# One written order for the query, value and gate heads of a DeltaNet layer on a Trainium2 core

## The chip, the core and the metric

The kernel runs on one core of one Trainium2 chip. Times are device microseconds (us) of one execution. The kernel before was run three times: 1217.61, 1218.7 and 1219.78, median 1218.7. The profile is of one more execution, recorded by the hardware profiler.

A core has five engines that work side by side, each with a queue of instructions that it takes strictly in order: TensorE (PE, matmuls; the loading of its stationary operand is shown apart as PEld), VectorE (DVE), ScalarE (ACT), GpSimd (POOL) and SyncE (SP, which here only issues DMA transfers; ScalarE issues some too). They meet through semaphores: an instruction whose input is not ready waits, and so does everything behind it on its queue. SBUF is the on-chip memory, 128 partitions wide; PSUM holds the matmul results.

## The reference, cut to what matters

The whole program is two layers on 512 latent and 256 context tokens of width 1024 (`D_MODEL`): a bidirectional gated DeltaNet layer and an attention layer. Only a part of the first is touched. There, the normalised tokens are projected, a convolution of width 5 over the tokens and a SiLU follow for queries, keys and values, and a gate z is projected without a convolution:

```python
p = u @ w_in
qkv = jax.nn.silu(centred_dwconv(p[..., :DN_CONV_DIM], conv_w))
z = p[..., DN_CONV_DIM:DN_CONV_DIM + DN_VAL_DIM]
...
q = jnp.repeat(l2_norm(q.reshape(b, l, DN_QK_HEADS, DN_HEAD_K)), rep, axis=2)
k = jnp.repeat(l2_norm(k.reshape(b, l, DN_QK_HEADS, DN_HEAD_K)), rep, axis=2)
v = v.reshape(b, l, DN_V_HEADS, DN_HEAD_V)
```

There are 8 query heads, 8 key heads, 16 value heads and 16 gate heads of 128 columns each. Then, per value head, per direction and per chunk of 64 tokens:

```python
a = jnp.where(strict, jnp.einsum('bhncd,bhnsd->bhncs', kb, kc) * decay, 0.0)
t_inv = lax.linalg.triangular_solve(eye + a, jnp.broadcast_to(eye, a.shape),
                                    left_side=True, lower=True, unit_diagonal=True)
...
qk = jnp.einsum('bhncd,bhnsd->bhncs', qc, kc) * decay
...
def step(s, xs):
    qk_i, qd_i, kd_i, u_i, w_i, gl_i = xs
    v_new = u_i - jnp.einsum('bhcd,bhde->bhce', w_i, s)
    o = jnp.einsum('bhcd,bhde->bhce', qd_i, s) + jnp.einsum('bhcs,bhse->bhce', qk_i, v_new)
    s = s * gl_i[..., None, None] + jnp.einsum('bhcd,bhce->bhde', kd_i, v_new)
    return s, o
```

So `t_inv`, the inverse of a unit lower triangular 64x64 block, is needed for every chunk, value head and direction, and `qk` likewise. Both can be computed before the recurrence over chunks begins.

## The kernel before, in words

The program runs in stages: the modulated norm and the key heads (to about 167 us); the **stage of the change** (167 to 602 us), which computes the query, value and gate heads and, beside them, all block inverses and all masked query-key products; the recurrence over 12 chunk steps (`products`, `solve`, `update`, L889 to L985); the output projection, the attention layer and the last norm.

**One head.** A head is a GEMM of a 1024x128 weight slice with the 1024x768 token matrix. The 32-bit product is built from high and low parts: `wh` and `wl` of the weight, `uh` and `ul` of the tokens, and three products `wh*uh`, `wh*ul`, `wl*uh`. That makes 24 matmuls of 512 latent columns and 24 of 256 context columns for each head (`gemm_T`, L342; the matmul is L349). `load_w` (L324) loads the slice with a DMA on SP (L329), ScalarE casts it to `wh` (L330), and VectorE or POOL subtracts to get `wl` (L331). For query and value heads `conv_silu` (L361) makes the convolution from the PSUM result: ScalarE writes the middle tap (L368), VectorE adds four taps (L371) for the latent columns and four for the context columns, ScalarE takes a tanh and VectorE completes the SiLU: L382 writes `sil_q` in two pieces, with the chunks placed in pairs, L376 writes `sil_v`. A gate head has no taps, only tanh and one VectorE instruction per part.

What follows differs. A **query** head (`q_head`, L531) is squared by ScalarE (`sq_q`, L499), TensorE sums the squares (`ss_q`, L504), and the head is stored to the DRAM buffer `q_d`. A **value** head (`v_head`, L762) is transposed by TensorE to tokens, copied by ScalarE into `vt`, and stored to `v_d` by a DMA on ScalarE's queue; this "tail" is held back by two heads (`turn_tails`). A **gate** head (`z_head`) is stored to `z_d`.

**The block inverses.** The tokens form six tiles t = 0 to 5 of 128 rows, each a pair of 64-row chunks. All of this runs in 32x32 sub-blocks. Per tile:

- *masked products* (`t_masked`, L585): load the keys `kk` (from `k_d`, which the key heads stored, L529) and the decay rows `df`; ScalarE makes the decays with 16 small instructions (L581) and one exponential (L582) for each direction v = 0, 1; TensorE forms the products of the keys, `G` (L604); VectorE masks them into `Gx` (L606) and multiplies with the decays (L562): `md` for the diagonal sub-blocks (128 partitions) and `mo` for the off-diagonal ones (two instructions of 32 partitions). VectorE transposes `md` to `L` (L626), so that the heads and directions lie on the partitions.
- *solve* (`t_solve`, L669): for two tiles together POOL inverts the 32x32 triangles column by column: 31 columns, each a product into `tmp` (L682) and a subtraction from `X` (L683), 93 of each in all.
- *join* (`t_join`, L691): VectorE transposes `X` back to `U` (two instructions, L698), TensorE makes `pp` from `mo` and `U` (64 small matmuls, L704), ScalarE negates it into `pn`, TensorE makes `pw`, and ScalarE copies all into `Tt`, of which there are two buffers in turn, and which is stored to `t_d`.
- *queries* (`t_queries`, L632): the products `GQ` of keys and queries, masked by VectorE and multiplied with the decays by POOL (12 products of 128x1024, all on POOL), stored to `qk_d`.

**What sets the order.** The stage is placed by the Tile scheduler: the program text gives an order, `issue_after` adds "not before" conditions, and the scheduler fills the engines' queues. The head loop (L784 on) emits q0 to q7, then the string `"z" * 5 + "vvz" * 8 + "zzz"`. Weights are split up to three heads ahead, for query heads on POOL, for all others on VectorE. Beside the heads a generator `pieces()` yields pieces of the inverses and query products, of which one is taken per query head, two per value head and three per gate head.

**Behind the stage.** The recurrence's order is written by hand already. Its first step loads on SP, in this order, `cT` from `t_d`, four pieces of `cv` from `v_d` (L878), three pieces of `cQK`, and the keys `ckt`. The first update of the state is the matmul `su` (L969), which reads `ckt`.

## Time and profile before

| | before |
|---|---|
| median of three runs | 1218.7 us (1217.61 to 1219.78) |
| the profiled execution's own time | 1220.96 us |
| its span in the profile | 1219.2 us |
| granted TensorE clock, mean | 0.978 |
| busy share of the span: PE / PEld / DVE / ACT / POOL | 94% / 76% / 66% / 60% / 47% |
| bytes moved by DMA | 208.73 MB, mean 171 GB/s |

The profile is a page of views and a trace that can be asked for more. "Busy" is the time in which an engine executes; waits and DMA issues do not count. Engine names with a q (ACTq, SPq) stand for the issue of transfers from that engine's queue. In a group of instructions `x24` is their count, after it come busy time and mean duration in ns, and behind the next bar the idle time of the engine just before them with what ended most of it. In a list of single instructions the first number is the start, the second the duration, and a bracket gives the idle time before it. The clock is the share of full speed that TensorE was granted: 0.50 is half speed.

### The profile page before, as it was taken

The numbers are of one execution on the slowest core, as the hardware profiler recorded it, in microseconds if no ns is written. First come the engines' busy times: TensorE is split into PE (matmuls) and PEld (weight loads), VectorE is DVE, ScalarE is ACT, GpSimd is POOL, SyncE is SP. The second block draws the span as 40 slices with busy tenths as digits, with TensorE's granted clock in tenths as the row PEclk, the third lists the DMA queues.
The fourth block names the chain that finished last, engine by engine and source line by source line (L and its number), as shares of the span: only waits on it lengthen the run. The fifth ranks groups of instructions, "written<-read, shape, count | busy, mean of one in ns | idle before, by whom it ended". The sixth has DMA issues, their size and how long they took to land. (4 is left out here: it accounts for less than half of the span.)

```text
span 1219.2 us, 27757 instructions
## 1 busy us (share of the span) xinstructions
PE 1144.4 (94%) x10739; PEld 928.9 (76%) x10739; DVE 800.2 (66%) x1734; ACT 731.5 (60%) x1945; POOL 579.1 (47%) x442
## 2 busy tenths in 40 slices
PE   4999999999789989899999999899999999999996
PEld 1677678888678877788856666688887889999884
DVE  2688565777879645675478888635556566566646
ACT  3344336675565678896268999686663236666731
POOL 0131114229999999830067568455753344230810
PEclk9999899999899998899999999999999999999998
DMA  9465986454436569752999999266672202101323
GB/s 335 137 227 169 338 258 191 130 166 155 132 111 178 162 187 280 235 177 98 295 267 242 260 270 250 76 223 190 217 233 98 70 26 80 52 19 53 104 69 87
DMA packets 171125, 208.73 MB, mean 171 GB/s; under 512 B 12497, under 2 KB 126322, under 8 KB 170226
## 3 DMA queue, kind: packets, MB, share of 16 engines
q1 hardware_dynamic: 151346, 197.02, 53.8%
q10 hardware_dynamic: 19648, 9.94, 2.9%
q8 instruction: 85, 1.39, 0.5%
q14 instruction: 46, 0.38, 0.1%
HBM read 166.16 MB, written 40.67 MB: 170 GB/s over the span
## 5 line engine op out<-in xcount | busy, mean ns | idle before, releaser
L918 POOL TENSOR_TENSOR S<-S,glb 128x512 f32<-128x512 f32 x80 | 81.7, 1043 | 122.0 <-PE ks L909 122.0
L1076 PE MATMUL po<-woh,y 128*128 128x512 f32 x384 | 130.0, 403 | 0.7 <-ACT y L1052 0.7
L349 PE MATMUL g_v<-uh,wh 128*128 128x512 f32 (+1 forms) x256 | 91.4, 357 | 14.8 <-DVE sil_v L376 14.8
L1025 POOL TENSOR_TENSOR wol<-wo,woh 128x1024 fp32r<-128x1024 f32 x32 | 77.1, 2411 | 55.6 <-ACT woh L1018 52.7
L683 POOL TENSOR_TENSOR X<-X,tmp 128x62 f32<-128x62 f32 (+15 forms) x93 | 95.8, 1031 | 6.5
L371 DVE SCALAR_TENSOR_TENSOR acc_v<-g_v,cwv,acc_v 128x510 f32<-128x510 f32 (+3 forms) x128 | 74.5, 610 | 33.9 <-ACT acc_v L368 32.3
L349 PE MATMUL g_z<-uh,wh 128*128 128x512 f32 (+1 forms) x256 | 88.6, 346 | 5.7 <-DVE sil_v L376 5.7
L682 POOL TENSOR_TENSOR tmp<-L,X 128x62 f32<-128x62 f32 (+15 forms) x93 | 89.0, 957 | 6.9
L349 PE MATMUL g_v<-ul,wh 128*128 128x512 f32 (+1 forms) x256 | 89.6, 350 | 0.0
L349 PE MATMUL g_v<-uh,wl 128*128 128x512 f32 (+1 forms) x256 | 88.7, 346 | 0.0
L349 PE MATMUL g_z<-ul,wh 128*128 128x512 f32 (+1 forms) x256 | 87.3, 341 | 0.0
L349 PE MATMUL g_z<-uh,wl 128*128 128x512 f32 (+1 forms) x256 | 87.1, 340 | 0.0
L1076 PEld LDWEIGHTS po<-woh,y 128*128 128x128 f32 x384 | 72.5, 189 | 16.0 <-ACT y L1052 0.9
L1076 PE MATMUL po<-wol,y 128*128 128x512 f32 x192 | 75.7, 395 | 0.9 <-POOL wol L1025 0.9
L349 PEld LDWEIGHTS g_v<-uh,wh 128*128 128x128 f32 x256 | 50.6, 198 | 21.6 <-DVE sil_v L376 15.5
L331 POOL TENSOR_TENSOR wl_k<-w_k,wh_k 128x1024 fp32r<-128x1024 f32 x8 | 19.3, 2415 | 94.6 <-ACT wh_k L330 94.6
L331 POOL TENSOR_TENSOR wl<-w,wh 128x1024 fp32r<-128x1024 f32 x8 | 19.4, 2426 | 83.6 <-ACT wh L330 83.6
L349 PEld LDWEIGHTS g_z<-uh,wh 128*128 128x128 f32 x256 | 49.2, 192 | 11.6 <-DVE sil_v L376 6.4
L331 DVE TENSOR_TENSOR wl<-w,wh 128x1024 fp32r<-128x1024 f32 x32 | 49.9, 1560 | 11.6 <-ACT wh L330 11.6
L1050 DVE SCALAR_TENSOR_TENSOR pt<-pt,og,z 128x128 f32<-128x128 f32 x96 | 34.4, 358 | 34.7 <-PE pt L1041 31.9
L909 PE MATMUL ks<-S,ck 128*64 128x256 f32 x352 | 55.2, 392 | 0.4 <-ACT o L915 0.4
L983 DVE TENSOR_TENSOR S<-su,S 128x512 f32<-128x512 f32 x80 | 51.5, 686 | 6.0 <-PE su L969 3.9
(375 smaller groups left out, 3397.4 us busy)
## 6 DMA issues: line engine op xcount, KB each, us to landing
aw<-in_ada_w SPq DMA_DIRECT2D x24, 1024.0 KB, 7.3
w<-in_dn_w_in SPq DMA_DIRECT2D x40, 512.0 KB, 4.6
wo<-in_dn_w_out SPq DMA_DIRECT2D x32, 512.0 KB, 3.3
cv<-v_d SPq DMA_DIRECT2D x48, 256.0 KB, 8.0
df<-gc_d SPq DMA_DIRECT2D x48, 128.0 KB, 2.8
z_d<-zs SPq DMA_DIRECT2D x16, 384.0 KB, 5.8
v_d<-vt ACTq DMA_DIRECT2D x16, 384.0 KB, 4.0
t_d<-Tt SPq DMA_DIRECT2D x6, 1024.0 KB, 5.1
```

What stands on the lines that cost most here:

```text
L331: split_at[0] = E.tensor_tensor(wl[:, :, :m], w[:, :, :m], wh[:, :, :m], ALU.subtract).ins
L349: mm = T.matmul(pg_[:m, :n], w[:, k, :m], u[:, k, c0:c0 + n], start=k == 0 and n_ == 0, stop=k == KT - 1 and n_ == 2)
L371: V.scalar_tensor_tensor(acc[:, c0 + lo:c0 + hi], ps[:, lo + j - 2:hi + j - 2], cwv[:, j, ct:ct + 1], acc[:, c0 + lo:c0 + hi], ALU.mult, A ...
L682: E.tensor_tensor(tv, bcast(L[:, :, j + 1:, j], 3, j + 1), bcast(X[:, :, j, 0:j + 1], 2, n), ALU.mult)
L683: E.tensor_tensor(X[:, :, j + 1:, 0:j + 1], X[:, :, j + 1:, 0:j + 1], tv, ALU.subtract)
L909: T.matmul(ks[r0:r0 + 64, w], kq[w][:, hh, r0:r0 + 64], St[hh][:, d], start=True, stop=True)
L918: G.tensor_tensor(St[hh], St[hh], bcast(g_, 3, P), ALU.mult)
L983: V.tensor_tensor(St[hh], sj, St[hh], ALU.add)
L1025: G.tensor_tensor(wl, raws.pop(n), halves[n][0], ALU.subtract)
L1050: V.scalar_tensor_tensor(pj, pj, og, raw(z, off, [[st_, 2], [1, 64]]), ALU.mult, ALU.mult)
L1076: T.matmul(acc[:, nh], y[i][:, j, :], ww[k][:, nh * 512:(nh + 1) * 512], start=h == 0 and x == 0, stop=h == VH - 1 and x == 2)
```

## The change

The change replaces the scheduler's placement of this stage by an order that is written out for all five queues (`tc.manual_schedule` over TensorE, VectorE, ScalarE, GpSimd and SyncE). The arithmetic stays the same.

- Time is cut into **slots**, one per head. The new order of heads is `"zzzzzqqzqqzqqvqqvvzvvzvzvvzvvzvzvvzvvzvz"`: five gates first, then queries mixed with gates and values, the last three heads being z14, v15, z15 (before: three gates).
- In slot n the loop emits: the load of the weights of head n+3; planned loads; the store of head n-2; planned TensorE work (`pe`); the latent GEMM of head n; copies of head n-2; the end of head n-1 (context taps, both SiLU parts, for queries the square); the split of the weights of head n+2 (POOL while n < 4, VectorE after); the context GEMM of head n; the turn of head n-1 on TensorE (sums of squares or transposes); planned middle work (`mid`: masks, mask products, turns); some columns of the solve on POOL, by a budget of 8.6 per slot; the beginning of head n (latent taps); late planned work (decays).
- Both SiLU parts of a query or value head n-1 lie in slot n. A gate's latent part now comes before its context part, and lies in its own slot.
- The key products `G` of tiles 0 to 5 stand in slots 1, 2, 5, 8, 11, 13; `L` is turned at the slots in `TURNED`; `U` at 18, 21, 26, 29, 34, 37, with `pp` ahead of the GEMM one slot later and `pw` two slots later; query products in slots 19, 22, 25, 28, 31, 34.
- *Larger pieces of mask products:* for v = 0 the off-diagonal product `mo` is one instruction over all 128 partitions, of which v = 1 then overwrites the blocks 0 and 3 in two instructions as before. Per tile there are three `mo` instructions instead of four.
- Of the twelve query products those of tiles 0 to 2 stay on POOL; the six of tiles 3 to 5 go to VectorE.
- There is one `Tt` buffer instead of two, `U` is one tile instead of two, and the decay rows have four buffers of one kind.

```diff
-    for Tt in Tts:
-        for b in range(4):
...
+    def decay(t, v, first, last):
+
+        df = dfs[t, v]
+        for h in range(first, last):
             S.activation(df[:, h], df[:, h], AF.Abs, scale=-1.0, bias=gcV[:, v, t, h:h + 1])
-        S.activation(df, df, AF.Exp, scale=-1.0)
...
+        if last == VH:
+            S.activation(df, df, AF.Exp, scale=-1.0)
...
+    def m_prod(t, v):
...
+        df, Gx, mo, md = dfs.pop((t, v)), Gxs[t], mos[t], mds[t]
+        decayed(V, md[:, v], df[:, :, 0:32], Gx[:, :, 0:32])
+        for r in ((slice(0, P),), (slice(0, 32), slice(96, P)))[v]:
+            decayed(V, mo[r], df[r, :, 32:64], Gx[r, :, 32:64])
...
-                for b in ((1, 2), (0, 3))[v]:
-                    r = slice(b * 32, b * 32 + 32)
-                    decayed(V, mo[r], df[r, :, 32:64], Gx[r, :, 32:64])
...
+    order = "zzzzzqqzqqzqqvqqvvzvvzvzvvzvvzvzvvzvvzvz"
+    heads = [(c, order[:n].count(c)) for n, c in enumerate(order)]
...
+    def decay_at(s, t, v):
+        at_slot(s, "late", decay, t, v, 0, 12)
+        at_slot(s + 1, "mid", decay, t, v, 12, VH)
+
+    POOL_FROM = 4
+    TURNED = (3, 4, 10, 12, 15, 18)
+    for t, (s, p0, p1) in enumerate(((1, 2, 2), (2, 3, 4), (5, 7, 8), (8, 10, 11), (11, 13, 14), (13, 16, 17))):
+        if t >= 2:
+            at_slot(s - 1, "sp", keys_loaded, t, False)
+            for v in range(2):
+                at_slot(s - 1, "sp", decay_rows, t, v, True)
+                decay_at(s + v, t, v)
+        at_slot(s, "pe", m_gram, t)
+        at_slot(s, "mid", m_masks, t)
+        at_slot(p0, "mid", m_prod, t, 0)
+        at_slot(p1, "mid", m_prod, t, 1)
+        at_slot(TURNED[t], "mid", m_turn, t)
+    at_slot(0, "sp", keys_loaded, 0, False)
+    at_slot(1, "sp", keys_loaded, 1, False)
+    for n in range(4):
+        at_slot(0, "sp", decay_rows, n // 2, n % 2, True)
+        at_slot(n, "late", decay, n // 2, n % 2, 0, VH)
+    for t, s in enumerate((18, 21, 26, 29, 34, 37)):
+        at_slot(s, "mid", j_turn, t)
+        at_slot(s + 1, "pe", j_first, t)
+        at_slot(s + 1, "mid", j_mid, t)
+        at_slot(s + 2, "pe", j_second, t)
+        at_slot(s + 2, "mid", j_end, t)
+        at_slot(s + 3, "sp", lambda t=t: dma(t_d[t], Tt))
+    for t, s in enumerate((19, 22, 25, 28, 31, 34)):
+        at_slot(s - 1, "sp", keys_loaded, t, True)
+        for v in range(2):
+            at_slot(s - 1, "sp", decay_rows, t, v, False)
+        at_slot(s, "pe", q_gram, t)
+        at_slot(s, "mid", q_masks, t)
+        for v in range(2):
+            decay_at(s + v, t, v)
+            at_slot(s + 1 + v, "mid", q_prod, t, v, G if t < 3 else V)
+            at_slot(s + 2 + v, "sp", q_store, t, v)
...
+    def head_begun(n):
+        if heads[n][0] == "z":
+            squash(n, 0)
+            silu(n, 0)
+        else:
+            taps(n, 0)
+
+    def head_ended(n):
+        c, h = heads[n]
+        if c == "z":
+            squash(n, 1)
+            silu(n, 1)
+            return
+        taps(n, 1)
+        squash(n, 0)
+        silu(n, 0)
+        squash(n, 1)
+        silu(n, 1)
+        if c == "q":
+            sq = sums[n] = ap_.tile([P, NT, P], F32, tag="tok", name=f"sq_{c}{h}").rearrange("p t k -> p (t k)")
+            S.activation(sq, sils[n], AF.Square)
...
+    written_p = tc.manual_schedule(engines={T.engine, V.engine, S.engine, G.engine, nc.sync.engine})
+    written_p.__enter__()
+    for n in range(3):
+        w_load(n)
+        if n < 2:
+            w_split(n, G)
+    for n in range(N + 3):
+        p_ = plan[n]
+        if 3 <= n + 3 < N:
+            w_load(n + 3)
+        run(p_["sp"])
+        if 2 <= n < N + 2:
+            head_stored(n - 2)
+        run(p_["pe"])
+        if n < N:
+            gemm_part(n, 0)
+        if 0 <= n - 2 < N:
+            head_copied(n - 2)
+        if 0 <= n - 1 < N:
+            head_ended(n - 1)
+        if n + 2 < N:
+            w_split(n + 2, G if n < POOL_FROM else V)
+        if n < N:
+            gemm_part(n, 1)
+        if 0 <= n - 1 < N:
+            head_turned(n - 1)
+        run(p_["mid"])
+        solve_some(n)
+        if n < N:
+            head_begun(n)
+        run(p_["late"])
+        if n == N - 1:
+            run(rsqrt_steps(rq.rearrange("p t h -> p (t h)"), 1.0))
...
-    work = pieces()
-    ahead = set()
-    order = "z" * 5 + "vvz" * 8 + "zzz"
...
-    for n_, (f_, h) in enumerate(heads):
-        for g_, h_ in heads[n_:n_ + 3]:
-            c_ = column[g_] + h_
-            if (g_, h_) not in ahead:
-                ahead.add((g_, h_))
-                split_ahead(c_, f"{c_}", G if g_ is q_head else V)
-        at[0] = n_
-        f_(h)
-        with tc.issue_after(split_at[0]), tc.issue_after(split_at[1]), tc.issue_after(at[1]), tc.issue_after(done[-2][0]), tc.issue_after(done[-2][1]):
-            for _ in range({q_head: 1, z_head: 3, v_head: 2}[f_]):
-                next(work, None)
```

## What the change was predicted to do

> **What bounds the kernel now.** I read the page first (span, shares, slices), then the windows of the stage that the change rewrites, then the timeline at TensorE's gaps there. All times are in us.
>
> ```profile
> span 1219.2 us, 27757 instructions
> ```
> ```profile
> 166.90:296.60 129.70, 129.70 (x1145) 110.24 (x1144) 89.52 (x164) 81.68 (x220) 52.02 (x45) 1.00 0.60 173
> 296.60:602.00 305.40, 276.40 (x3254) 240.12 (x3256) 202.89 (x280) 202.07 (x501) 214.86 (x186) 0.96 0.59 182
> 360.00:400.00 40.00, 35.51 (x566) 31.18 (x566) 38.56 (x41) 23.53 (x46) 36.38 (x29) 0.96 0.54 149
> 366.00:369.40 3.40, 3.05 (x7) 2.47 (x8) 3.40 (x4) 2.21 (x4) 3.24 (x3) 0.50 0.86 228
> 505.90:512.70 6.80, 6.10 (x14) 4.79 (x15) 6.25 (x8) 5.47 (x19) 3.31 (x3) 0.50 0.68 219
> ```
> ```profile
> 506.60 0.79 PE L349 MATMUL g_v<-uh,wh 128*128 128x512 f32 x1 [3.12 <-DVE sil_v L376]
> ```
>
> A window's columns are its length, the busy time of PE, PEld, DVE, ACT and POOL, the granted clock, and DMA. TensorE bounds this stage: it is busy for all of 129.70 while the first 13 heads (q0 to q7, z0 to z4) run. Over the other 27 heads it idles 305.40 - 276.40 = 29.0, and 4% of the clock is missing, 12, part of it inside the gaps; I count 10. So 39 is all that a better order can win here. The reader is to see two more things: a gap waits for VectorE's silu (sil_v), and in the one window where VectorE is full (38.56 of 40) TensorE starves (35.51). The clock was 0.50 for 6.8 after the gap of 3.12.
>
> **The change part by part.** Every queue's order is now written. In slot n TensorE runs the GEMM of head n and, behind it, the turn of head n-1: the sums of a query's squares, or a value's transposes. VectorE runs the four taps of head n-1's context columns, its silu, the weights' subtraction for head n+2, the "mid" work (masks, mask products, turns), then the four taps of head n's latent columns (for a gate, one silu).
>
> *TensorE's work* keeps its amount:
>
> ```profile
> 197.08 0.39 PE L349 MATMUL g_q<-uh,wl 128*128 128x512 f32 x1
> 197.31 0.39 PE L349 MATMUL g_q<-uh,wh 128*128 128x512 f32 x1
> 199.06 0.28 PE L349 MATMUL g_q<-uh,wh 128*128 128x256 f32 x1
> 199.18 0.28 PE L349 MATMUL g_q<-ul,wh 128*128 128x256 f32 x1
> 206.53 0.87 PE L504 MATMUL ss_q<-ones,sq_q 128*64 128x1 f32 x24
> 287.06 1.10 PE L604 MATMUL G<-kk 128*32 128x64 f32 x64
> 518.66 1.29 PE L704 MATMUL pp<-U,mo 32*32 32x32 f32 x128
> ```
>
> From start to start a latent matmul takes 0.23 and a context one 0.12: a head is 24 x 0.228 + 24 x 0.12 = 8.35. With 0.8 for sums, about as much or a little less for transposes, 1.1 for a pair of G products and 1.25 for each join product, slots 5 to 18 hold 130.6 and slots 19 to 39 hold 205.4.
>
> *The start.* G of tile 0 now stands on TensorE straight behind z0 and the last key head's transposes (before, two query heads lay between), and all of z1 behind it. It needs k_d, which that key head's store completes.
>
> ```profile
> 181.42 1.02 DVE L518 TENSOR_TENSOR kt<-tr_k,kss 128x512 f32<-128x512 f32 x2
> 188.18 0.86 ACT L526 COPY kb<-kb 128x512 f32<-128x512 f32 x2 [0.55 <-PE kb L524]
> 189.07 0.37 ACTq L529 DMA_DIRECT2D k_d<-kb  x1
> 187.25 6.29 SPq L589 DMA_DIRECT2D kk<-k_d  x2
> DMA to landing us min/median/max: 2.7/4.6/5.1
> ```
>
> (The last row is that of tile kk.) kt is there at 182.4, z0 ends near 181.6 (where q0 ends now), the transposes near 183.2, the store goes out at 183.8. The second key load ended its issue at 187.25 + 6.29 = 193.5, 4.1 from the store's start at 189.07 to its own start; then 4.6 to land: 183.8 + 4.1 + 4.6 = 192.5, against a TensorE free at 183.2. Less G's own first half, 8.8 idle (2.7 to land gives 6.9; twice the store's time gives 13). A gap of that size halves the clock: 6.8 x 0.5 less what lies in the gap, 2.3 taken. Sum 11; z4 ends near 230. VectorE is nearly idle in these five slots: a gate head gives it one silu and, until head 5, POOL subtracts the weights.
>
> *Slots 5 to 18: query heads, masks and values.*
>
> ```profile
> 183.22 2.04 DVE L371 SCALAR_TENSOR_TENSOR acc_q<-g_q,cwv,acc_q 128x254 f32<-128x254 f32 x4 [0.78 <-ACT acc_q L368]
> L371 DVE SCALAR_TENSOR_TENSOR acc_q<-g_q,cwv,acc_q 128x511 f32<-128x511 f32 x12 | 8.9, 738 | 0.1
> 179.50 0.76 DVE L382 SCALAR_TENSOR_TENSOR sil_q<-g_q,acc_q 128x256 f32<-128x256 f32 x2
> 186.28 0.48 DVE L382 SCALAR_TENSOR_TENSOR sil_q<-g_q,acc_q 128x128 f32<-128x128 f32 x2
> L376 DVE SCALAR_TENSOR_TENSOR sil_v<-g_v,acc_v 128x512 f32<-128x512 f32 x16 | 10.9, 682 | 4.3 <-ACT g_v L374 4.2
> L376 DVE SCALAR_TENSOR_TENSOR sil_v<-g_v,acc_v 128x256 f32<-128x256 f32 x16 | 6.7, 419 | 3.4 <-ACT g_v L374 3.4
> L331 DVE TENSOR_TENSOR wl<-w,wh 128x1024 fp32r<-128x1024 f32 x32 | 49.9, 1560 | 11.6 <-ACT wh L330 11.6
> L499 ACT ACTIVATE sq_q<-sil_q 128x768 f32<-128x768 f32 x7 | 5.9, 836 | 0.5 <-DVE sil_q L382 0.5
> L330 ACT CAST wh<-w 128x1024 fp32r<-128x1024 f32 x35 | 36.5, 1043 | 7.1 <-PE g_v L349 4.1 <-DMA w<-in_dn_w_in 1.9 <-PE g_z L349 1.0
> L562 DVE TENSOR_TENSOR mo<-df,Gx 32x512 f32<-32x512 f32 x24 | 28.0, 1167 | 2.7 <-ACT Gx L607 2.4
> L562 DVE TENSOR_TENSOR md<-df,Gx 128x512 f32<-128x512 f32 x12 | 11.1, 928 | 6.1 <-ACT df L582 6.0
> L606 DVE TENSOR_TENSOR Gx<-G,masks 128x128 f32<-128x128 f32 x12 | 3.4, 283 | 0.8 <-PE G L604 0.8
> L626 DVE STREAM_TRANSPOSE L<-md 128x1024 f32<-128x1024 f32 x6 | 13.6, 2272 | 2.4 <-POOL tmp L682 2.3
> L698 DVE STREAM_TRANSPOSE U<-X 128x1024 f32<-128x1024 f32 x12 | 24.6, 2120 | 0.0
> L581 ACT ACTIVATE df<-df,gcV 128x64 f32<-128x64 f32 x189 | 47.5, 337 | 6.2 <-DMA df<-gc_d 6.2
> L582 ACT ACTIVATE df<-df 128x1024 f32<-128x1024 f32 x12 | 12.7, 1057 | 0.0
> ```
>
> A VectorE slot behind a query is 2.05 + 1.25 for taps and silu; then a wait of 2.0, since ScalarE's square (0.84) and the cast that the subtraction needs (1.04) both come after that silu; 1.56; the mid work M; 4 x 0.78 = 3.1. That is 10.1 + M. Behind a value the square is absent: 8.3 + M. Behind a gate: 5.5 + M. Where the current head is a gate, the last 3.1 is 0.7. M is 2.1 or 3.3 for a half of the mask products (the first of a pair as one instruction of 128 partitions, 0.93 + about 1.17; the three narrow ones were 1.17 each), 0.6 for masks, 2.3 for L, 4.2 for U. Slots 6 to 18 come to 147 (10.1, 9.8, 9.5, 10.1, 12.1, 9.5, 12.4, 12.8, 11.7, 12.4, 12.2, 11.7, 12.6); in slots 6 and 9 ScalarE's decays (12 x 0.25, then 4 and the exponential, 2.1) add 1.5 each: 150. TensorE needs 121. It lets VectorE run late by at most 3.6, as the square of head n-1 ends 4.75 into slot n and its sums are due at 8.35. So 29 - 3.6 = 25 of idle, 2 to 4 per slot from slot 10. If only VectorE's busy time counted, slots 10 to 18 would hold 95.6 against 83.1: 9.
>
> *The joins.* U is turned in slots 18, 21, 26, 29, 34, 37, and the first join product stands ahead of the next head's GEMM. From a value's silu it is 0.35 + 1.56 + 4.2 = 6.2 to U's end. With VectorE on time the silu ends 4.4 before the GEMM: 1.2 of wait; with VectorE just late enough, 5.6. In slot 18 L's 2.3 comes on top. Laid out slot by slot, ScalarE's 8 copies into Tt ahead of the next taps included, I get 7.9, 5.0, 3.3, 4.5, 3.3, 5.7: 30 (floor 9.5).
>
> *The end.* v15 is now the last head but one (now three gates follow it), and its transposes are TensorE's last work. Their rows must reach v_d and come back.
>
> ```profile
> v_d<-vt ACTq DMA_DIRECT2D x16, 384.0 KB, 4.0
> ```
> ```profile
> 583.93 1.98 SPq L878 DMA_DIRECT2D cv<-v_d  x2
> 604.22 1.04 PE L969 MATMUL su<-vd,ckt 64*64 64x256 f32 x16
> DMA to landing us min/median/max: 5.6/6.4/8.6
> ```
>
> (The last row is that of tile ckt.) On SP the last cQK and ckt stand behind the two loads of v_d[1]. With the stage's TensorE end at 230 + 130.6 + 25 + 205.4 + 30 = 621: copies 1.0, store 4.0, two loads' issue 2.0, a cQK issue 0.6, ckt 6.4: su starts at 635. Now it starts at 604.22.
>
> *The rest, at nothing.* POOL's columns (8 to 9 a slot, as planned) end some slots before U needs them; if not, U waits and the joins grow. Of POOL's twelve query products six go to VectorE, 1.8 each (twice md), in slots 29 to 36, inside the join sum; two subtractions more go there too, 3.1, in slots 4 and 5 where it is idle. SP loads each weight three slots ahead; one Tt buffer has at least two slots between its store and its next copy.
>
> **Sum.** 635 - 604 = +31 on the profiled execution of 1220.96 (span 1219.2), which lies 2.3 above the median 1218.7: 1250.
>
> By the Trainium skill, "TensorE: Matmul & The Clock Gate", Part 1, the clock falls after an idle window of about 3.4. Here 3.12 was enough. By that rule only four of the six join gaps would slow the clock, and the slow rival below would be 1259, not 1264.
>
> **The rivals.**
> - *Faster:* VectorE stays within its 3.6 of lateness, so the 25 goes and the joins fall to 9.5: 31 - 25 - 20.5 = -14, 1204. For it: 129.70 of 129.70 busy, with VectorE at 69%. Against it: 35.51 with VectorE at 96%, and the wait for the square, which the order fixes. It decides at a lateness of 3.6 in slots 10 to 18.
> - *Half:* the square's wait is hidden, 9 in place of 25, and the joins cost 20: +5, 1224.
> - *Clock:* each join gap also costs 2.3 of half clock that no lateness absorbs: +14 more, 1264. Against it: while VectorE is late, a slower TensorE only shortens the next wait.
> - *No change:* the terms meet the 39 exactly.
>
> **How the numbers follow.** Forecast 0.48 (its own range 1234 to 1260), half 0.21, clock 0.11, no change 0.03, faster 0.17. What measurement can tell from no change is about 0.2%. Slower 0.80, same 0.03, faster 0.17. Low end: 9 for 25, floor joins, a start of 9: 31 - 16 - 20.5 - 2 = -8, 1211. High end: clock, and a start of 15: 1269.
>
> **What would show it.** Right: TensorE idle about 9 before G of tile 0; sums of squares waiting for sq_q in slots 9 to 16, 2 to 4 each; join products waiting for U, 3 to 8 each; the first su near 635. Wrong: VectorE on time at slot 18 (z4's end plus 131), join gaps near 1, or G of tile 0 not waiting.

## The result, and the profile after

The changed kernel takes 1277.89 us in the median of four runs (1267.13 to 1281.11), the kernel before 1218.64. The ratio is 1.047 with a 95% interval of 1.0408 to 1.0533. The direction was forecast, the size was not: 1250 with a range of 1211 to 1269. The profiled execution took 1276.98, 56.0 longer in its span than that of the kernel before.

First the page of the changed kernel: span, busy time per engine, and the granted clock in 40 slices.

```profile
span 1275.2 us, 27658 instructions
PE 1156.2 (91%) x10739; PEld 940.4 (74%) x10739; DVE 816.1 (64%) x1736; ACT 732.8 (57%) x1945; POOL 554.6 (43%) x430
PEclk9999899999998998989879999999999999999998
```

TensorE's instructions are as many as before. What has grown is its waiting, and the clock dips where it waits. Next the windows, cut where the prediction cut its sum (columns: length, busy time of PE, PEld, DVE, ACT, POOL, clock, DMA): to z4's end, to the end of slot 18, to TensorE's last work in the stage, and from there to the first `su`.

```profile
166.90:230.60 63.70, 54.83 (x446) 44.67 (x449) 27.01 (x48) 32.81 (x94) 14.43 (x9) 0.92 0.65 186
230.60:385.00 154.40, 138.38 (x1139) 120.78 (x1138) 125.67 (x178) 87.20 (x229) 112.47 (x104) 0.96 0.48 133
385.00:643.00 258.00, 221.03 (x2815) 194.55 (x2814) 153.62 (x220) 164.63 (x397) 115.42 (x105) 0.91 0.55 161
643.00:657.70 14.70, 4.58 (x48) 2.79 (x49) 2.56 (x12) 2.21 (x5) 0.00 (x0) 0.62 0.96 286
```

TensorE idles 8.9, 16.0 and 37.0 us in the first three. The prediction's work of 130.6 and 205.4 for the second and third leaves 138.38 - 130.6 = 7.8 and 221.03 - 205.4 = 15.6. That is half clock for the most part, but not all of it: in the stretches at half clock TensorE was busy for 13.6 and 28.0, which cost 6.8 and 14.0. The other 1.0 and 1.6 are work that the forecast counted too low. The groups of TensorE's instructions over the stage say what it waited for (last column: idle time just before them, and its cause).

```profile
L642 PE MATMUL pp<-U,mo 32*32 32x32 f32 x768 | 9.5, 213 | 18.0 <-DVE U L633 17.0 <-DVE KQ L687 1.0
L678 PE MATMUL GQ<-kq_4q 128*64 128x64 f32 x32 | 1.8, 274 | 9.8 <-ACT Tt L668 9.8
L839 PE MATMUL ss_q<-ones,sq_q 128*64 128x1 f32 x192 | 7.1, 200 | 8.5 <-ACT sq_q L829 8.3
L571 PE MATMUL G<-kq_0m 128*32 128x64 f32 x64 | 2.2, 313 | 8.3 <-DMA kq_0m<-k_d 8.3
L375 PE MATMUL tr_v<-ident,sil_v 128*128 128x128 f32 x96 | 13.9, 283 | 7.6 <-DVE sil_v L801 7.6
L678 PE MATMUL GQ<-kq_3q 128*64 128x64 f32 x32 | 2.2, 320 | 7.1 <-DMA w_z<-in_dn_w_in 4.3 <-ACT Tt L668 2.7
L1050 PE MATMUL pr<-cv,cT 64*64 64x128 f32 x44 | 3.8, 426 | 5.2 <-DMA cv<-v_d 4.4 <-ACT vn L1052 0.7
L1076 PE MATMUL pq<-vn,cQK 64*64 64x128 f32 x16 | 1.8, 436 | 4.9 <-DMA cQK<-qk_d 4.9
L678 PE MATMUL GQ<-kq_2q 128*64 128x64 f32 x32 | 1.4, 227 | 2.0 <-DMA kq_2q<-q_d 2.0
```

The G wait, the sums and transposes, the join products `pp` and the end are all there, as forecast. The waits of the query products `GQ`, 18.9 in sum, are not in the forecast at all. Two single matmuls from the timeline, and ScalarE's copies just before the second:

```profile
502.54 0.37 PE L678 MATMUL GQ<-kq_3q 128*64 128x64 f32 x2 [2.75 <-ACT Tt L668]
546.51 0.48 PE L678 MATMUL GQ<-kq_4q 128*64 128x64 f32 x4 [9.84 <-ACT Tt L668]
```
```profile
543.18 1.03 ACT L758 CAST wh_v<-w_v 128x1024 fp32r<-128x1024 f32 x1
544.12 2.34 ACT L668 COPY Tt<-pw 32x512 f32<-32x512 f32 x4
```

`pw`, the first and the second half of `GQ` share a PSUM tag of two buffers. In slots 28 and 31 the query products stand straight behind a `pw`, so the second half waits until ScalarE has copied that `pw` into `Tt`. In ScalarE's written order these copies stand behind two tanh and a cast of the same slot. The clock falls as well: two of the three longest stretches at half clock between slots 19 and 39 begin inside waits of `GQ` (at 496.32 and 540.70).

```profile
496.32:506.56 10.24, 5.14 (x39) 4.28 (x40) 5.96 (x12) 4.16 (x7) 9.61 (x9) 0.50 0.67 232
540.70:550.94 10.24, 4.43 (x24) 3.64 (x25) 5.55 (x12) 4.16 (x7) 0.00 (x0) 0.50 0.58 211
```

With the 3.4 after the wait of tile 2's `GQ` (462.2 to 465.6), half clock behind `GQ` costs 6.5 of the 14.0.

### The profile page after: what moved, and what is told of

Same layout as the page of the kernel before. It is cut to its first block, busy times and chain, and to the rows that moved or that the text cites. A ratio compares the mean times of both kernels' runs of the same rounds, so it can differ in the third digit from the quotient of the medians.

```text
span 1275.2 us, 27658 instructions
## 1 busy us (share of the span) xinstructions
PE 1156.2 (91%) x10739; PEld 940.4 (74%) x10739; DVE 816.1 (64%) x1736; ACT 732.8 (57%) x1945; POOL 554.6 (43%) x430
## 5 line engine op out<-in xcount | busy, mean ns | idle before, releaser
L771 PE MATMUL g_v<-uh,wh_v 128*128 128x512 f32 (+1 forms) x256 | 91.6, 358 | 0.0
L771 PE MATMUL g_z<-uh,wh_z 128*128 128x512 f32 (+1 forms) x256 | 90.0, 351 | 0.0
L771 PE MATMUL g_v<-ul,wh_v 128*128 128x512 f32 (+1 forms) x256 | 89.2, 349 | 0.0
L771 PE MATMUL g_v<-uh,wl_v 128*128 128x512 f32 (+1 forms) x256 | 88.8, 347 | 0.0
L771 PE MATMUL g_z<-ul,wh_z 128*128 128x512 f32 (+1 forms) x256 | 87.8, 343 | 0.0
L771 PE MATMUL g_z<-uh,wl_z 128*128 128x512 f32 (+1 forms) x256 | 87.6, 342 | 0.0
L771 PEld LDWEIGHTS g_v<-uh,wh_v 128*128 128x128 f32 x256 | 50.8, 198 | 6.7 <-issue 0.2
L771 PEld LDWEIGHTS g_v<-ul,wh_v 128*128 128x128 f32 x256 | 50.8, 198 | 5.7
L771 PEld LDWEIGHTS g_v<-uh,wl_v 128*128 128x128 f32 x256 | 50.5, 197 | 6.1
L1027 DVE SCALAR_TENSOR_TENSOR r<-ks,negV,cv 128x128 f32<-128x128 f32 x176 | 52.0, 344 | 4.5 <-DMA cv<-v_d 2.3
```

What stands on the lines that cost most here:

```text
L771: T.matmul(ps[:, :m], w[:, k], u[:, k, c0:c0 + m], start=k == 0 and n_ == 0, stop=k == KT - 1 and n_ == 2)
L1027: V.scalar_tensor_tensor(r[:, 2 * j + i], ks[:, 0, i], negV[:, visit, t, h:h + 1], v[:, h], ALU.mult, ALU.add)
```

## The experiments

Each kernel is the changed kernel with the edit shown. Medians are of four runs (twelve for e14, e15 and e17), and ratios are to runs of the kernel before on the same chip. As the changed kernel's own runs spread over 14 us, a difference of a few us in a median is not read without the trace behind it: the ratio of the changed kernel itself is known to 1.0408 to 1.0533. "Idle" is TensorE's, from the same view as above, in the profiled execution.

### The query products' buffers and the joins

**e4: query products of tiles 3 and 4 in other slots.**

```diff
-    for t, s in enumerate((19, 22, 25, 28, 31, 34)):
+    for t, s in enumerate((19, 22, 25, 29, 32, 34)):
```

> Only the query products of tiles 3 and 4 move with their loads, from slots 28 and 31, where the join products pw stand just ahead of them, to slots 29 and 32. Theory: there are two PSUM banks for pw, GQ0 and GQ1; GQ1 waits until ScalarE has copied pw into Tt, and that copy stands late in ScalarE's slot. The waits of 10.0 (tile 4) and 2.9 (tile 3) go to under 1, with some 6 us of half clock: the time falls by 13 to 19, to 1258 to 1264. Rival: what is late is the load of the keys and queries on SP; then the waits follow the products to the new slots and the time stays within 4 us of 1277.

Measured: 1258.51, ratio 1.0332 (1.0303 to 1.0360), 19 below the changed kernel.

```profile
L678 PE MATMUL GQ<-kq_3q 128*64 128x64 f32 x32 | 1.2, 225 | 0.0
L678 PE MATMUL GQ<-kq_4q 128*64 128x64 f32 x32 | 1.2, 225 | 0.0
```

Both waits are gone and did not follow to the new slots. The buffers are the cause where the profile names `Tt` (12.6 of the 18.9). The 4.3 that it puts on a transfer went too, and this run does not say why: the last of the keys' loads had been issued at 484.9, 13.8 us before that matmul, and these loads took 5.6 to 7.0 to land.

**e3: the first join product behind the latent GEMM.**

```diff
-        at_slot(s + 1, "pe", j_first, t)
+        at_slot(s + 1, "pe2", j_first, t)
-        at_slot(s, "pe", q_gram, t)
+        at_slot(s, "pe2" if t < 2 else "pe", q_gram, t)
...
             gemm_part(n, 0)
+        run(p_["pe2"])
```

> Only the first join products pp move, behind the latent GEMM of their slot, 5.5 us later (in slots 19 and 22 the query products behind them go along). Theory: pp waits for the turned U, at most 6.7 us; the six waits of 19.3 us in sum fall under 3, and the half clock that four of them bring goes too (some 8 us): the time falls by 20 to 27, to 1250 to 1257. Rival: ScalarE, whose copies into Tt now start 5.5 later, hands the delay on, to pw, to the taps or to the query products' bank; then the waits of GQ and tr_v grow and under 10 us are won.

Measured: 1284.16, ratio 1.0523 (1.0489 to 1.0557). `pp`'s waits fell as expected, the time did not: the rival held.

```profile
L642 PE MATMUL pp<-U,mo 32*32 32x32 f32 x768 | 7.8, 193 | 1.4 <-DVE U L633 1.4
L661 PE MATMUL pw<-pn,U 32*32 32x32 f32 x768 | 8.5, 193 | 8.8 <-issue 8.8
L678 PE MATMUL GQ<-kq_4q 128*64 128x64 f32 x32 | 1.8, 274 | 11.8 <-ACT Tt L668 11.8
L1051 PE MATMUL pr<-cv,cT 64*64 64x128 f32 x32 | 2.9, 430 | 12.8 <-DMA cv<-v_d 12.1 <-ACT vn L1053 0.7
```

The wait at `pp` goes from 18.0 to 1.4, and `pw`, the query products and the start of the recurrence take it over. By the written order all of these stand behind ScalarE's negation and copies, which now wait for the later `pp`; the profile names them for the query products (`Tt`), but names no releaser for `pw`.

**e8: a whole slot between `U` and `pp`, and query products where no join product stands.**

```diff
-    for t, s in enumerate((18, 21, 26, 29, 34, 37)):
+    for t, s in enumerate((18, 21, 26, 29, 33, 36)):
...
-        at_slot(s + 1, "pe", j_first, t)
-        at_slot(s + 1, "mid", j_mid, t)
-        at_slot(s + 2, "pe", j_second, t)
-        at_slot(s + 2, "mid", j_end, t)
-        at_slot(s + 3, "sp", lambda t=t: dma(t_d[t], Tt))
+        at_slot(s + 2, "pe", j_first, t)
+        at_slot(s + 2, "mid", j_mid, t)
+        at_slot(s + 3, "pe", j_second, t)
+        at_slot(s + 3, "mid", j_end, t)
+        at_slot(s + 4, "sp", lambda t=t: dma(t_d[t], Tt))
...
-    for t, s in enumerate((19, 22, 25, 28, 31, 34)):
+    for t, s in enumerate((19, 22, 25, 30, 34, 37)):
...
-            at_slot(s + 1 + v, "mid", q_prod, t, v, G if t < 3 else V)
+            at_slot(s + 1 + v, "mid", q_prod, t, v, V if t == 3 else G)
```

> U is turned as before (tiles 4 and 5 one slot earlier), but pp, pw, their copies and the store stand one slot later, and the query products stand in slots where no join product does (19, 22, 25, 30, 34, 37), those of tiles 4 and 5 on POOL. Theory: with a slot between VectorE's turn and TensorE's use, and with no join product ahead of a query product in the two banks, both kinds of waits go: pp 18 us to under 3, GQ 18.8 us to under 4, and with the half clock of these gaps (some 12 us) the time falls by 35 to 46, to 1231 to 1242. Rival: VectorE or ScalarE is late in these slots by its work, and the waits turn up at the transposes of the values; then under 25 us are won.

Measured: 1256.04, ratio 1.0290 (1.0262 to 1.0319): 22 won, not 35.

```profile
L642 PE MATMUL pp<-U,mo 32*32 32x32 f32 x768 | 7.7, 193 | 0.0
L1050 PE MATMUL pr<-cv,cT 64*64 64x128 f32 x64 | 4.7, 391 | 13.3 <-DMA cv<-v_d 12.6 <-ACT vn L1052 0.7
```

The 18.0 at the joins is gone entirely, and the query products' waits fall to 8.5. TensorE's last GEMM ends 24 earlier (618.2 for 642.3). Part of it is given back at the end, where `pr` now waits 13.3: tile 5's query products lie later, and SP stands at their stores (20.6 at the longest) with the recurrence's loads behind. The rival holds in part too: the wait of the values' transposes for `sil_v` rises from 7.6 to 11.1.

### Slots 10 to 18

**e2: the whole split of the weights first.** In the loop, `w_split(n + 2, ...)` moves ahead of `head_ended(n - 1)`.

> Only the split of the weights (cast and subtraction) moves, ahead of the end of head n-1 on ScalarE and VectorE. Theory of the prediction: in slots 10 to 18 VectorE loses 2 us per query head by waiting for the square and then the cast; without that wait TensorE's waits for sq_q and for sil_v up to slot 18 fall from 17 us to 7 to 9, and the time by 8 to 12. Rival: VectorE's busy time alone sets the pace (its mask products take up to 2.4 us while POOL works, 0.7 otherwise); then the waits only change their names and the time stays within 4 us of 1277.

Measured: 1274.15, ratio 1.0448 (1.0422 to 1.0475). The waits for `sq_q` and `sil_v` are 15.5 in sum, 16.1 in the changed kernel: in the written order the subtraction now stands in the way of the taps instead. By itself this spoke for the rival.

**e6: the turn of a head one slot later.**

```diff
-        if 0 <= n - 1 < N:
-            head_turned(n - 1)
+        if 0 <= n - 2 < N:
+            head_turned(n - 2)
```

> Only the turn of a head (sums of squares, transposes) moves, one slot later, with a third buffer for the SiLU results (the query products' masked tiles take over dead buffers to make room). Theory of the prediction: VectorE is late in slots 10 to 18 by the square and the cast, and TensorE waits for it only because the turn stands so close behind; with a whole slot more the waits for sq_q and sil_v fall from 16 us to under 4, and with their half clock (some 5 us) the time falls by 14 to 20, to 1257 to 1263. Rival: VectorE's busy time is the limit there; then the lateness adds up and GEMMs wait for PSUM banks instead, or the first join products wait longer, and under 6 us are won.

Measured: 1274.79, ratio 1.0438 (1.0404 to 1.0472). In the window 300 to 375:

```profile
L772 PE MATMUL g_v<-uh,wh_v 128*128 128x512 f32 (+1 forms) x48 | 17.1, 356 | 5.9 <-DVE sil_q L808 5.9
L772 PE MATMUL g_q<-uh,wh_q 128*128 128x256 f32 (+1 forms) x40 | 14.2, 356 | 5.6 <-DVE sil_v L802 5.4 <-DVE sil_q L808 0.2
L840 PE MATMUL ss_q<-ones,sq_q 128*64 128x1 f32 x96 | 3.5, 199 | 0.0
```

The sums wait no more, but the GEMMs do, for PSUM buffers that VectorE has not emptied. A lateness that grows in every slot is not cured by a longer lead. What makes it grow, work or waits, was still open.

**e9: ScalarE's cast earlier.**

```diff
         taps(n, 1)
+        if n >= 4:
+            w_cast(n + 3)
         squash(n, 0)
```

`w_cast` is `S.copy(wh, w)` alone; the subtraction stays where it was.

> Only ScalarE's cast of the weights moves, for slots behind a query or value: ahead of the two tanh and the square, while ScalarE waits for VectorE's taps anyway. VectorE's work and its order stay. Theory A (waits): VectorE falls behind in slots 10 to 18 because it waits 0.5 us (value) to 2 us (query) per slot for that cast; without it TensorE's waits for sq_q and sil_v fall from 16 us to 3 to 6, and the time by 12 to 18 with its half clock, to 1259 to 1265. Theory B (busy time): VectorE's instructions alone fill these slots, as the GEMMs that waited for sil_v when the turn was moved speak for; then 10 us or more of the waits stay and the time falls by under 7.

Measured: 1253.72, ratio 1.0264 (1.0236 to 1.0291), 24 below the changed kernel, for one ScalarE instruction moved ahead of two tanh and a square. First VectorE's subtractions and TensorE's sums in the changed kernel, then in e9:

```profile
L759 DVE TENSOR_TENSOR wl_v<-w_v,wh_v 128x1024 fp32r<-128x1024 f32 x16 | 20.9, 1307 | 8.8 <-ACT wh_v L758 8.8
L759 DVE TENSOR_TENSOR wl_q<-w_q,wh_q 128x1024 fp32r<-128x1024 f32 x7 | 9.3, 1328 | 11.4 <-ACT wh_q L758 11.4
```
```profile
L768 DVE TENSOR_TENSOR wl_v<-w_v,wh_v 128x1024 fp32r<-128x1024 f32 x16 | 20.1, 1254 | 0.4 <-ACT wh_v L761 0.4
L768 DVE TENSOR_TENSOR wl_q<-w_q,wh_q 128x1024 fp32r<-128x1024 f32 x7 | 10.2, 1453 | 0.3 <-ACT wh_q L761 0.3
L850 PE MATMUL ss_q<-ones,sq_q 128*64 128x1 f32 x192 | 6.9, 199 | 3.7 <-ACT sq_q L840 3.7
L642 PE MATMUL pp<-U,mo 32*32 32x32 f32 x768 | 8.7, 204 | 12.2 <-DVE U L633 12.0 <-DVE KQ L687 0.2
```

This is nearer to Theory A: about half of the lateness was VectorE's wait for the cast. It cost 11.4 over seven query heads, 1.6 each, and 0.55 per value head. Without it the sums and transposes wait 7.9 in place of 16.1, which lies between A's 3 to 6 and B's 10. The time falls by more than A said, because the waits behind fall too: as VectorE reaches `U` earlier, `pp` goes from 18.0 to 12.2, and the query products' waits go from 18.9 to 13.0. Of the 7.9 that are left, no run separates VectorE's work from the waiting for POOL that its busy time holds (see the last section).

**e16: one part of the change undone, the wide mask product.**

```diff
-        for r in ((slice(0, P),), (slice(0, 32), slice(96, P)))[v]:
+        for r in ((slice(32, 64), slice(64, 96)), (slice(0, 32), slice(96, P)))[v]:
```

> The changed kernel with one part undone: the off-diagonal mask product of v = 0 again as two instructions of 32 partitions in place of one of 128. Theory: VectorE gets one instruction of 0.7 to 2.4 us more per tile, 7 us in all in slots 2 to 16, where it is late anyway: the time rises by 2 to 6 us against 1277. Rival: the one wide instruction costs as much as two narrow ones, because it runs beside POOL's: no difference beyond 3 us.

Measured: 1284.12, ratio 1.0527 (1.0482 to 1.0571), 6 above the changed kernel. The intervals of the two ratios overlap, so the time alone shows no difference. The trace agrees with the theory: the waits of the query sums are 12.3 (8.5 with the wide product) and those of the transposes 8.6 (7.6). So the larger pieces probably help, by an amount that these runs do not fix.

### The start

**e1: key products of tiles 0 and 1 one slot later.**

```diff
-    for t, (s, p0, p1) in enumerate(((1, 2, 2), (2, 3, 4), (5, 7, 8), (8, 10, 11), (11, 13, 14), (13, 16, 17))):
+    for t, (s, p0, p1) in enumerate(((2, 2, 2), (3, 3, 4), (5, 7, 8), (8, 10, 11), (11, 13, 14), (13, 16, 17))):
-    at_slot(1, "sp", keys_loaded, 1, False)
+    at_slot(2, "sp", keys_loaded, 1, False)
```

> Only the key products of tiles 0 and 1 move, from slots 1 and 2 to slots 2 and 3 (the first mask products of tile 1 to slot 3). Theory: the start stall is the wait of G for the last key head's store and its reload, and it shifts everything behind it. G of tile 0 then waits under 1 us in place of 4.9 + 3.7, the 10.2 us of half clock there go, z4 ends near 219 us in place of 230.5, and the time falls by 11, to about 1266. Rival: the later slots are late for another reason (VectorE, POOL's columns) and take the gain back: z4 ends near 219 but the time stays within 4 us of 1277.

Measured: 1272.67, ratio 1.0455 (1.0403 to 1.0508). The waits of G became 3.3 and 5.4 (tile 1, whose loads stood behind tile 0's products): no less in sum.

**e7: keys of both tiles loaded in slot 0, G behind the latent GEMM of slot 2.** The keys of a tile share one buffer, so that two tiles fit; `m_gram` of tile 0 runs behind `gemm_part(2, 0)`, that of tile 1 in slot 3.

> The keys of one tile share one buffer, so that the keys of tiles 0 and 1 are both loaded in slot 0; G of tile 0 stands behind the latent GEMM of slot 2, G of tile 1 at slot 3. Theory: the start stall is the round trip of the last key head; moved past it, both G wait under 1 us (before 4.7 + 3.6; in the run with one slot more 3.3 + 5.4, where the loads of tile 1 stood behind tile 0's products), the half clock of 10.2 us goes, and the time falls by 9 to 12, to 1265 to 1268. Rival: later slots take it back; then z4 ends 10 us earlier and the time stays within 4 us of 1277.

Measured: 1277.03, ratio 1.0470 (1.0426 to 1.0515). First TensorE's groups to 235 us, then ScalarE's timeline:

```profile
L776 PE MATMUL g_z<-uh,wh_z 128*128 128x512 f32 (+1 forms) x79 | 28.9, 366 | 8.0 <-DVE sil_z L804 8.0
L576 PE MATMUL G<-kq_0m 128*32 128x64 f32 x64 | 1.1, 220 | 0.0
```
```profile
199.48 3.93 ACT L563 ACTIVATE df_0m<-df_0m,gcV 128x64 f32<-128x64 f32 x16 [13.43 <-DMA df_0m<-gc_d]
```

G of tile 0 no longer waits (that of tile 1 waits 1.8), and a gate's GEMM waits 8.0 instead. (The next expectation calls that a wait for weights; by these rows it is PSUM.) On SP the decay rows stand behind the key loads, now of two tiles, which wait for the last key head's store. ScalarE stands 13.4 at the first decay, with z1's tanh behind it (204.40), so VectorE's SiLU is late and the GEMM finds no free buffer. One late transfer stalled the stage over three queues.

**e10: SP's order changed too.** Decay rows of tile 0 in slot 0 ahead of the keys, keys in slot 1 behind the weights of head 4, decay rows of tile 1 in slot 2.

> As the run with G behind slot 2's latent GEMM, but SP's order changes too: the decay rows of tile 0 before the keys, the weights of head 4 before the keys, the decay rows of tile 1 behind the weights of head 5. Theory: what stalls the start is SP's queue, on which the key loads wait for the last key head's store (until 188 to 191 us) with decay rows and weights behind them; moving only the products made a gate's GEMM wait 8.0 us for its weights. Now neither G nor a GEMM waits over 1 us up to slot 5, and the time falls by 9 to 12, to 1265 to 1268. Rival: the gain at the start is eaten by later slots, as all of slots 5 to 39 run after VectorE: z4 ends 10 us earlier and the time stays within 4 us of 1277.

Measured: 1271.27, ratio 1.0421 (1.0402 to 1.0440), 6.6 below the changed kernel, which by itself is within its spread. G of tile 2, which follows right on z4, now starts 6.6 earlier than in the changed kernel (first of e10, then of the changed kernel):

```profile
L576 PE MATMUL G<-kq_2m x64: 216/219/243, 223.9 to 226.9; 128*32 128x64 f32 x64
```
```profile
L571 PE MATMUL G<-kq_2m x64: 219/219/243, 230.5 to 231.4; 128*32 128x64 f32 x64
```

TensorE's last GEMM then ends 5.2 earlier (637.1 for 642.3), and the profiled span is 5.3 shorter. So a gain at the start is kept to the end, against the rival. It is smaller than expected: G of tile 1 still waits 3.7, for ScalarE's copy of tile 0's `G` into `Gx`, which frees the PSUM buffer, and G of tile 2 waits 1.9 for its keys.

### The end

**e5: v15 a slot earlier** (the order ends in `vvvzz` in place of `vvzvz`).

> Only the order of the last heads changes: v15 comes a slot earlier, behind v14, and two gates end the stage. Theory: the recurrence starts late because v15's rows go to v_d and back after TensorE's last matmul, with the other loads of the first step queued behind on SP. From TensorE's last GEMM to the first su the time falls from 15.4 us to 4 to 7, the half clock there (17 us) goes too, and the time falls by 9 to 14, to 1263 to 1268. Rival: the stores ahead of these loads on SP (t_d of tile 5, z15) hold them as long; then the time stays within 4 us of 1277.

Measured: 1275.49, ratio 1.0446 (1.0402 to 1.0489). From the last GEMM (641.8) to `su` (653.6) 11.8, for 15.4. The loads went out late all the same, from 636.61 on. The longest of SP's waits between 575 and 645 (us in total, times, longest):

```profile
SPq L733 <- ACT Tt L668: 35.3, 2, 27.5
```

SP stood at the store of `Tt` of tile 5 until 635.77, since ScalarE makes the last copies into `Tt` in slot 39; z14's store and the first loads came right behind it.

**e11: the last stores on ScalarE's queue.**

```diff
-            dma(z_d[h], sils[n])
+            (dma if n < N - 2 else nc.scalar.dma_start)(z_d[h], sils[n])
...
-        at_slot(s + 3, "sp", lambda t=t: dma(t_d[t], Tt))
+        at_slot(s + 3, "sp", lambda t=t: (dma if t < 5 else nc.scalar.dma_start)(t_d[t], Tt))
```

> v15 a slot earlier, as before, and the last stores (z14, z15, t_d of tile 5) on ScalarE's queue in place of SP's. Theory: with v15 earlier the first loads of the recurrence still went out late, from 636.6 us, because they stood on SP behind stores that wait for the last heads; off that queue they go out some 12 us earlier, the first su follows TensorE's last GEMM by 2 to 5 us (15.4 in the changed kernel, 11.8 with v15 earlier), and the time falls by 11 to 16 against 1277, to 1261 to 1266. Rival: ScalarE's own queue delays those stores or the copies of the recurrence; then under 5 us are won.

Measured: 1275.61, ratio 1.0460 (1.0436 to 1.0484); again 11.8. The longest of SP's waits between 607 and 645 (us in total, times, longest):

```profile
SPq L993 <- DMA v_d<-vt: 19.9, 2, 13.8
```

The issues of `cv` now wait for stores on another queue, among them loads of `v_d[0]`, whose stores had landed long before. In the trace each of these transfers waits on the very semaphore that it raises, and eight semaphores go round among all transfers of SP and ScalarE. So a load waits for whichever store had its semaphore last.

**e13: z15's store behind the first loads.** Its SiLU goes to a buffer of its own, and the store is issued after `load_step(0)`.

> v15 a slot earlier, and the store of the last gate z15 issued on SP behind the loads of the recurrence's first step (its result lies in a buffer of its own; the query products' masked tiles take over dead buffers to make room). Theory: the first loads go out late because of what stands before them in the written order: SP issues in order, and each transfer also waits until an earlier one that used the same semaphore (some eight before it, on any queue) has landed; that is why moving the stores to another queue changed nothing. With z15's store behind them the loads go out while the last GEMM runs: from TensorE's last GEMM to the first su 4 to 7 us (11.8 with v15 earlier alone), and the time falls to 1262 to 1270. Rival: the loads wait for memory that the inverses' last buffers hold (Tt, U, mo); then su still comes 10 us or more behind the last GEMM.

Measured: 1274.42, ratio 1.0444 (1.0395 to 1.0493); from the last GEMM (638.3) to `su` (650.3) 12.0. The loads of `cv` went out at 636.45, behind the store of `Tt` of tile 5 (632.26, for which SP had waited 26.3), and took 12.0 in the median to land (8.8 in the kernel before, which issued them 18 us ahead of its last GEMM's end). Neither theory is settled by it: z15's store no longer stood ahead of the loads, but that of `Tt` did, and then the loads were slower.

### All together

**e12: e8, e9, e10 and e11 together**, with tile 5's query stores on ScalarE's queue.

> All together: joins a slot later and query products in free slots, SP's order at the start, the early cast, v15 earlier with the last stores on ScalarE's queue. Theory: the losses are separate and add: the stage's idle time, 72 us in the changed kernel and 30 before, falls to 8 to 15, its half clock to under 10 us lost, su comes at 575 to 590, and the time is 1194 to 1210, under the 1219 of the kernel before. Rival: VectorE or ScalarE sets the pace once TensorE no longer waits elsewhere; then over 25 us of idle stay and the time is 1215 to 1240.

Measured: 1237.49, ratio 1.0130 (1.0088 to 1.0171). Of the 59 us over the kernel before, 40 are undone. In the profiled execution 39 us of idle are left up to the first `su`, 72 in the changed kernel; the last GEMM ends at 599.4, but `su` comes 16.5 later. The time and the idle time are the rival's, not the theory's; but the idle time is spread over many waits (12.0 at query products, 8.5 at `pr`, 8.4 at sums and transposes), and no run shows one engine setting the pace.

**e14: the same with e13 in place of e11**, tile 5's query stores back on SP, `U` of tiles 4 and 5 turned in slots 32 and 35, their query products in slots 33 and 36, keys two slots ahead, G of tile 1 behind slot 3's latent GEMM, tile 1's query products on VectorE, and a budget of 9.2 in place of 8.6 per slot for POOL's columns. What each of these gives by itself was not run.

> All parts together as before (1237), with the z15 store behind the first loads, joins of tiles 4 and 5 and their query products one slot earlier, keys loaded two slots ahead, G of tile 1 behind slot 3's latent GEMM, the query products of tile 1 on VectorE. Theory: the remaining losses are separate too. The wait from the last GEMM to su falls from 16.5 us to 4 to 8, GQ's waits from 12 to under 5, G's from 5.8 to under 2, and half clock with them: su at 588 to 598, the time 1207 to 1220, at or under the kernel before. Rival: POOL's solve now ends too late for U of tile 4, or VectorE falls behind in slots 30 to 36: then pp or tr_v wait over 10 us and the time stays at 1225 to 1240.

Measured: 1220.24, ratio 0.9996 (0.9972 to 1.0020). The theory held but for the end. The windows from 166.9 to the last GEMM and on to `su`, first of e14, then of the kernel before:

```profile
166.90:581.00 414.10, 398.42 (x4388) 346.41 (x4387) 300.82 (x438) 284.01 (x720) 251.72 (x220) 0.99 0.60 178
581.00:594.30 13.30, 4.76 (x49) 2.79 (x49) 3.11 (x15) 1.56 (x3) 0.00 (x0) 0.58 0.99 264
```
```profile
166.90:602.00 435.10, 406.10 (x4396) 350.36 (x4398) 292.40 (x443) 283.75 (x720) 266.88 (x230) 0.97 0.60 180
602.00:604.20 2.20, 1.50 (x48) 1.25 (x52) 1.34 (x6) 1.08 (x3) 0.00 (x0) 1.00 1.04 257
```

A written order does win in the stage: it ends 21 us earlier (17 and 18 in the next two runs), with 15.7 idle for 29.0 and the clock at 0.99. But 11.1 of that go in the hand-over (13.3 for 2.2), where the DMA engines are full (0.99, but 1.04 in the kernel before too), and 5.0 in the recurrence (181.2 for 176.2 from the first `su` to the output projection), for a reason that no run shows. The 4.9 that are left between the two profiled executions (1216.07 and 1220.96) do not show in the medians.

**e15: e14, tile 5's query stores on ScalarE's queue, and a gate moved to slot 13. e17: e14, tile 5's query products on VectorE.**

> The run with all parts, with two changes: the stores of tile 5's query products on ScalarE's queue, since SP waited until 578.2 us for the last of them with the first loads behind it, and one gate moved from slot 21 to slot 13 in place of a value, to give VectorE room ahead of slot 18. Theory: the first loads go out about 4 us earlier and land as much earlier (9 to 12 us after their issue, as the transfers are then limited by bandwidth), and 3 to 6 us of the 8.4 us of waits for sq_q and sil_v go: the time falls by 5 to 10, to 1210 to 1215, below the kernel before. Rival: the recurrence's start is bound by its transfers (the DMA engines are full there), so that it starts when they are done and no order helps: the time stays within 3 us of 1220.

> The first run with all parts but z15's late store and the rest (1220), with one change: the two query products of tile 5 on VectorE in place of POOL. Theory: there SP stood at the last of their stores until 578.2 us, because POOL's product of 2.4 us came late, and the recurrence's first loads went out at 579; on VectorE, 1.2 us each, the store goes out at 572 to 574 and the loads at 574 to 576, su comes 3 to 5 us earlier, and the time falls to 1214 to 1218. Rival: the loads land when the DMA engines have moved all that is queued, so that su stays 13 us behind the last GEMM and the time within 2 us of 1220.

Measured: 1219.97, ratio 1.0011 (0.9992 to 1.0031), and 1218.90, ratio 0.9999 (0.9977 to 1.0021). Both the same as the kernel before. (e17 is e14 with that one change; its expectation describes the base otherwise.) In neither did the first loads go out earlier (`cT` at 585.8 and 583.9, in e14 at 581.3): in e15 SP then stood 6.3 at z14's store for VectorE's SiLU, in e17 8.3 at the store of `Tt` and 3.0 at that of the query product. So the question that e17 was to tell, order or bandwidth, stays open.

## Why the prediction was wrong in size

By its own steps, forecast and measured, in us after the kernel before's place or as given:

| step | forecast | measured |
|---|---|---|
| start: idle, clock; z4's end | 8.8, 2.3; 230 | 8.9, about 2; 230.5 |
| slots 5 to 18: idle, clock; end | 25, 0; 385.6 | 16.0, 6.8; 385 |
| slots 5 to 18, 19 to 39: work | 130.6, 205.4 | 131.6, 207.0 |
| joins, idle | 30 | 18.0 |
| query products, idle | 0 | 18.9 |
| slots 19 to 39: clock | 0 | 14.0 |
| TensorE's end in the stage | 621 | 643 |
| from there to `su` | 14 | 14.7 |
| recurrence to the output projection | 0 | 2.4 |

*The start* was right in size and too narrow in cause. The wait for the key round trip is there to a tenth, but e7 shows that the same late transfer holds ScalarE through the decay rows. In the changed kernel the second half of G starts at 193.0, and ScalarE's first decay, with z1's tanh behind it, at 195.3 after a wait of 11.0. So the step explained only one of two paths of about equal length.

*Slots 5 to 18* had the mechanism right and their end by luck in part: VectorE is late from slot 10 on, but the idle time was overstated by 9.0, and half clock (6.8) and work (1.0) were left out, which nearly cancel. e9 shows half of the cause: with the cast's wait gone 7.9 of the 16.1 are left, near the floor of 9 that the rival *half* worked out from busy time alone.

*The joins* were the right mechanism, mis-sized: 6.4 in slot 19 for 7.9, but 1.0 to 1.8 in three of the six for 3.3 to 4.5.

*The failed step* is "The joins" and what follows it, which went through TensorE's order in slots 19 to 39 for `pp` alone. Its sum gave the query products 1.1 us each and no wait, though they stand behind `pw` in two slots, in a PSUM tag of two buffers whose emptying lies in "mid", behind the tanh and the cast of the same slot. The working counted ScalarE's eight copies into `Tt` only as a delay of the taps. What the runs showed in its place: waits of 18.9 at the query products and 6.5 of half clock behind them, for 0. e4 shows the price by itself: with two of them moved off the `pw`, 19 of the 28 us by which the forecast fell short are gone. Of the 18.9, 12.6 are ScalarE's late copies; the cause of the 4.3 stays open, and 2.0 are a load of the queries.

*The clock* was a rival at 0.11, turned down because "while VectorE is late, a slower TensorE only shortens the next wait". That fits slots 10 to 18, where clock and idle time cancelled. In slots 19 to 39 VectorE has room (153.62 busy of 258) and absorbs no half clock: 14.0 came on top, 6.5 of it behind the query products and 7.5 behind the joins.

Together: -12.0 at the joins, +18.9 at the query products, +14.0 for the clock, +1.6 for work, +0.7 at the end and +2.4 in the recurrence make 25.6 of the 27.9 between 1250 and 1277.9; the rest is mainly that the medians differ by 59.3 and the profiled executions by 56.0. The *faster* rival, that a written order brings TensorE to its floor, was right in part for a kernel that was not built: e14's stage is 21 us shorter, with 15.7 of idle left, and its time is the same as before.

## What to carry to other kernels

In a written order, follow every shared buffer, not only every operand: for each PSUM tag list who holds it, which instruction empties it, and what stands ahead of that instruction on its queue. Put the small instruction that others wait for (here a cast of 1 us) where its engine waits anyway, as it costs nothing there and cost 24 us elsewhere in this kernel. And look behind the end of the rewritten stage: the scheduler had slipped the next stage's loads in between the last stores, 18 us ahead of the last GEMM's end, and a written SP queue takes that away.

## What the runs showed of the hardware

Short gaps cost clock, if they fall badly. In the changed kernel a gap of 2.01 was followed by half clock (timeline and window):

```profile
461.36 0.36 PE L678 MATMUL GQ<-kq_2q 128*64 128x64 f32 x5 [2.01 <-DMA kq_2q<-q_d]
462.20:465.60 3.40, 3.40 (x9) 2.62 (x9) 2.81 (x6) 1.37 (x2) 3.16 (x4) 0.50 1.11 240
```

In e14 a gap of 2.69 was not followed by it (the clock stayed at 1.00 until 372):

```profile
365.85 0.33 PE L375 MATMUL tr_v<-ident,sil_v 128*128 128x128 f32 x1 [2.69 <-DVE sil_v L818]
```

So between 2.0 and 2.7 the length alone does not decide here. Where the gap lies matters too. In these traces the clock changes on a grid of 3.41 us. The gap of 2.01 lies inside one stretch of that grid, the gap of 2.69 across the border of two (first the changed kernel, then e14):

```profile
458.78:462.19 3.41, 1.40 (x33) 1.22 (x34) 3.27 (x6) 1.06 (x2) 3.17 (x5) 1.00 1.07 269
361.15:364.56 3.41, 2.01 (x17) 1.81 (x16) 3.23 (x7) 0.60 (x1) 3.07 (x3) 1.00 1.07 308
364.56:367.98 3.42, 2.13 (x39) 1.90 (x40) 3.42 (x5) 1.89 (x5) 0.00 (x0) 1.00 0.53 131
```

TensorE idles 2.01 in the first, 1.40 and 1.29 in the others. In the profiles of all nineteen kernels, from 200 to 640 us, each of the 136 stretches at full clock with over 1.85 idle was followed by half clock, and none of the 1906 with under 1.13; between the two both happened. The Trainium skill, "TensorE: Matmul & The Clock Gate", Part 1, gives an idle window of about 3.4 us that runs freely, whenever work starts. The grid agrees with the free running; that 2.01 sufficed shows that the window need not be idle throughout. The prediction's sentence by that rule had four of six join gaps slow the clock. Measured it was three, those of 3.40 to 6.42, while those of 1.0 to 1.8 did not; the gap of 2.01 shows that it is no rule of length alone.

The same product took VectorE 0.68 to 2.41 us in the changed kernel, by what POOL was doing when it started (VectorE's product, then POOL's instruction, twice):

```profile
293.40 2.41 DVE L533 TENSOR_TENSOR mo<-df_3m,Gx 128x512 f32<-128x512 f32 x1
292.84 2.43 POOL L600 TENSOR_TENSOR L<-L,bball 128x1024 f32<-128x1024 f32 x1 [9.69 <-DVE L L598]
327.60 0.68 DVE L533 TENSOR_TENSOR mo<-df_4m,Gx 128x512 f32<-128x512 f32 x1
327.07 1.81 POOL L608 MEMSET X<- 128x2048 f32 x1
```

The long product ends at 295.81, 0.54 after POOL's product of two SBUF tiles; the short one ran beside a POOL instruction that only writes. The thirty products `md` and `mo` of this trace sort the same way: the twenty that start while a POOL product or subtraction runs end 0.54 to 0.55 after it, and the ten others take 0.67 to 0.69. The twenty lose 21.5 us in all, which the profile counts as VectorE's busy time. The Trainium skill, "SBUF — State Buffer", section "SBUF: two separate sides", says that a VectorE instruction with two SBUF inputs and a POOL instruction that reads SBUF exclude each other for their whole length. The trace agrees with it on VectorE's side. What the stage would gain by keeping POOL's solve away from these products was not run.
